# Hybrid two-layer trunk: the first inputs regrouped into one array, fewer and wider first transfers, other first instructions

## The chip, the cores and the metric

The kernel runs on one core of one Trainium2 chip. The metric is device time of one launch in microseconds (us). TensorE is called PE below, VectorE DVE, ScalarE ACT, GpSimd POOL, and SyncE, which issues the transfers, SP.

## The reference

Two layers. Each normalises x, multiplies it with one wide input matrix, runs three kinds of heads on the columns of that product and maps their outputs back by a second matrix into the residual. The sequence has 256 rows, the model 1024 columns; the input matrix has 4360 columns.

```python
def hybrid_layer(x, norm_w, w_in, conv_w, conv_b, gate_bias, ret_norm_w, mlstm_norm_w, w_out):
    h = rmsnorm(x, norm_w)
    proj = jnp.matmul(h, w_in).astype(jnp.float32)
    ...
    (aq, ak, av, ag, bq, bk, bv, bg, cq, ck, cv, co, cg, ci, cf) = jnp.split(proj, cuts, axis=-1)
    ya = moba_attention(split_heads(aq, A_HEADS), ...)   # causal softmax with ALiBi, 8 heads of 64
    ya = merge_heads(ya) * jax.nn.silu(ag)
    yb = retention(rotate(bq, pos), rotate(bk, pos), bv) # 4 heads, decay in place of softmax
    yb = head_norm(yb, ret_norm_w) * jax.nn.silu(bg)
    qk = jax.nn.silu(causal_dwconv(jnp.concatenate([cq, ck], axis=-1), conv_w, conv_b))
    ...
    yc = mlstm(...)                                      # 4 heads, gated matrix memory
    yc = head_norm(yc, mlstm_norm_w) * jax.nn.silu(cg)
    y = jnp.concatenate([ya, yb, yc], axis=-1)
    return x + jnp.matmul(y, w_out)

def reference(x, ...):
    for layer in range(DEPTH):                           # DEPTH = 2
        x = hybrid_layer(x, ...)
    return rmsnorm(x, final_norm_w)
```

## The kernel before

Everything is held in float32. Each operand of a large product is split in two parts that PE multiplies at its fast rate: a rounded part (`hi` of a weight, `xh` of x) and the rest (`lo`, `xl`). Three products, `hi*xh`, `hi*xl` and `lo*xh`, then stand for one. ACT writes the rounded part, DVE subtracts it from the original to get the rest.

x lies transposed: 128 partitions, eight row groups k = 0 to 7 of 256 columns each (the tile `px`, behind 80 columns of small parameters). The weights come in 23 chunks a layer, in the order of use, each some 1 MB, into three `raw` buffers; ACT and DVE split each into one of three `hi` and `lo` buffers. Chunks 0 and 1 (the first four q heads and k heads of the attention) are handled apart: their products for one row group k can start when x's group k and the 256 columns of each chunk that belong to k are there. That is the head of the kernel: 96 products of 256 columns, 12 for each k.

The program's order is written by a small planner, `Sched`, at build time. Each stage (`loader`, `splitter`, `norm`, `project`, the evacuations) is a Python generator; the planner advances the one whose next instruction could start first by its own cost table, and so fixes the order on every engine. Where an instruction is given as `A(...) + V(...)` (the helper `CP`, a copy), the planner picks ACT or DVE by which would end first. The buffers are acquired and released in planner order.

The parts that matter here, with the lines of the profile: `loader` (transfers; the helper `D` on L288 issues them on SP), `first_x` and `first_w` (the split of the first x and weights; ACT on L265, DVE on L259), `norm(0)` (ACT squares pairs of x groups into `t512` buffers, DVE adds them up), `project` (the products; L280), and the preamble on L359 to L372 (memsets, one ACT instruction, two PE products of a zeroed `sb` buffer, whose results nobody reads). `loader` sends the head in 15 transfers: for the row groups 0, 1, 2-3, 4-5, 6-7 one of x and one of each chunk. Behind them on SP stand chunk 2 in two halves, the first table, chunk 3 and so on.

Of the kernel before, what the change touches and what calls it, by code (L numbers as in the profile page):

```python
# [10 lines left out]
F32 = mybir.dt.float32  # L11
# [5 lines left out]
S = 256  # L17
# [36 lines left out]
W_SIZES = [(k1 - k0) * len(c) for _, c, k0, k1 in CHUNKS] + [2048] * 4  # L54
W_OFFS = np.concatenate([[0], np.cumsum(W_SIZES)]).tolist()
W_TOTAL = W_OFFS[-1]


P_NW, P_CW, P_CB, P_GB, P_YW = 0, 16, 48, 56, 72
# [168 lines left out]
@with_exitstack  # L228
def trunk(ctx: ExitStack, tc: tile.TileContext, xp: bass.AP, w: bass.AP, fn: bass.AP,
          tab: bass.AP, out: bass.AP):  # L230
# [65 lines left out]
    def acq(tag):  # L296
        return ("acq", tag)
# [7 lines left out]

    px = sb_tile([128, P_N + KT * S], "px")
    pr = px[:, :P_N]
    x = px[:, P_N:].rearrange("p (k t) -> p k t", t=S)
    tb = sb_tile([128, T_N], "tb")
# [15 lines left out]
    gi = sb_tile([4, 2, S], "gi")  # L325
    on_a = sb_tile([128, 2, 512], "on_a")
    on_b = sb_tile([128, 2, 256], "on_b")
    hc = sb_tile([128, 2, 256], "hc")
    rrow = sb_tile([128, S], "rrow")
# [19 lines left out]
    sb_pool("lo", 3, [128, 2112], F32R)  # L349
    sb_pool("t512", 6, [128, 512])  # L350
    sb_pool("st", 7, [128, 512], F32R)
# [33 lines left out]
    def loader():  # L385
        for i in range(NL):
            l, c = divmod(i, NW)
            n = W_SIZES[c]
            o = l * W_TOTAL + W_OFFS[c]
            if i == 1:  # L390
                continue
            t = yield acq("raw")
            raws[i] = t
            if i < 2:
                if i == 0:
                    t1 = yield acq("raw")
                    raws[1] = t1
                    for a, b in ((0, 1), (1, 2), (2, 4), (4, 6), (6, 8)):
                        o1, o2 = P_N + a * S if a else 0, P_N + b * S
                        e = yield D((o2 - o1) * 512 / 360.0, px[:, o1:o2], xp[:, o1:o2])  # L400
                        for k in range(a, b):
                            sc.set(E("x0", k), e + 1100)
                        for m in range(2):
                            e = yield D((b - a) * 364, (t, t1)[m][:, a * 256:b * 256],
                                        w[:, o + m * 2048 + a * 256:o + m * 2048 + b * 256])
                            for k in range(a, b):
                                sc.set(E("rawk", m, k), e + 1100)
                continue
# [12 lines left out]
        sc.spawn(last_in(), 2)  # L421

    def split_x(l, k):
        wk = pr[:, P_NW + l * 8 + k:P_NW + l * 8 + k + 1]
        yield A(xh[:, k, :], x[:, k, :], AF.Copy, scale=wk)
# [7 lines left out]

    def first_w(m, k):
        yield wait(E("rawk", m, k))
        a = slice(k * 256, (k + 1) * 256)
        yield A(his[m][:, a], raws[m][:, a], AF.Copy)
        t = yield V("tensor_tensor", los[m][:, a], raws[m][:, a], his[m][:, a].bitcast(F32), op=OP.subtract)
        sc.set(E("wk", m, k), t)

    def splitter():
# [3 lines left out]
        for k in range(KT):  # L445
            sc.spawn(first_x(k), -3)
            for m in range(2):
                sc.spawn(first_w(m, k), -2)
        for m in range(2):
            for k in range(KT):  # L450
                yield wait(E("wk", m, k))
            sc.release("raw", raws.pop(m), E("wk", m, KT - 1).time)
        for i in range(2, NL):
# [19 lines left out]
    def norm(l):  # L473

        ss = None
        for k in range(0, KT, 2):
            for z in (k, k + 1):
                yield wait(E("x0", z) if l == 0 else E("res", l - 1, z))
            sq = yield acq("t512")
            yield A(sq, x[:, k:k + 2, :].rearrange("p a t -> p (a t)"), AF.Square)  # L480
# [87 lines left out]
    def project():  # L568
        for l in range(DEPTH):
# [3 lines left out]
            while c < len(CHUNKS):  # L573
# [23 lines left out]
                elif name[1] in "qk":  # L597
# [10 lines left out]
                    hv = [his[q][:, :2048].rearrange("p (k c) -> p k c", k=KT) for q in ii]  # L608
                    lv = [los[q][:, :2048].rearrange("p (k c) -> p k c", k=KT) for q in ii]
                    for k in range(KT):  # L610
                        yield wait(E("x", l, k))
                        for z in range(m):
                            yield wait(E("wk", z, k) if i == 0 else E("w", i + z, k // 4))
                            for t in range(2):
                                cs = slice(t * 128, (t + 1) * 128)
                                for q, (a, b) in enumerate(((hv[z], xh), (hv[z], xl), (lv[z], xh))):
                                    e = yield M(ps[z][:, t * 256:(t + 1) * 256], a[:, k, cs], b[:, k, :],
                                                k + t + q == 0, k == KT - 1 and q == 2)
                    for z, q in enumerate(ii):
# [591 lines left out]
```

## Time and profile before

| | |
|---|---|
| median of three runs (lowest, highest) | 302.06 us (301.41, 302.4) |
| the profiled execution's own time | 301.41 us |
| its span in the trace | 299.6 us |
| PE busy | 291.0 us, 97% of the span |
| DVE busy | 257.7 us, 86% |
| ACT busy | 196.6 us, 66% |
| bytes moved | 48.58 MB, 162 GB/s over the span |

The span runs from the first to the last instruction that the profiler saw; the launch's own time has 1.8 us around it. PE products are pipelined, so that the recorded durations overlap: the distance between two starts tells how fast PE goes, not the duration of one. The same holds, by less, for ACT and DVE.

### The profile page before, as it was taken

To read this page: it belongs to the slowest core of one execution; us is meant where nothing else is said; L and a number is where in the kernel's file an instruction comes from. 1 tells how busy PE (TensorE), PEld (TensorE's weight loads), DVE (VectorE), ACT (ScalarE), POOL (GpSimd) and SP (SyncE) were. 2 spreads that over 40 slices of the span, in tenths; PEclk is the share of its full clock that TensorE was granted. 3 is DMA by queue.
4 is the path that set the end of the run, shared out by engine and by line. 5 is a ranking of instruction groups with operands and counts; after the bars stand their busy time and mean duration, and the time that the engine had idled before them with its cause. 6 is when DMAs were issued, how large, how long until landed. Compare 5 with 4: busy or idle time off the path is not lost.

```text
span 299.6 us, 4795 instructions
## 1 busy us (share of the span) xinstructions
PE 291.0 (97%) x1792; PEld 258.2 (86%) x1792; DVE 257.7 (86%) x549; ACT 196.6 (66%) x341; POOL 15.3 (5%) x19
## 2 busy tenths in 40 slices
PE   8899999999999999999999999999999999999991
PEld 6798989888989888899988898988899988888881
DVE  3969999999999997985679999999999999956353
ACT  5958997889448539644666699779555265845332
POOL 6000000000002002000020000000002002000010
PEclk9999999999999999999999999999999999999997
DMA  6999456574710560754317663446541624330003
GB/s 200 374 398 352 153 174 223 184 258 143 238 45 0 161 240 22 249 174 148 136 19 264 205 222 125 156 142 219 203 142 45 237 67 173 123 131 0 2 0 140
DMA packets 9095, 48.58 MB, mean 162 GB/s; under 512 B 1008, under 2 KB 1904, under 8 KB 4080
## 3 DMA queue, kind: packets, MB, share of 16 engines
q1 hardware_dynamic: 9072, 48.28, 46.7%
q8 instruction: 14, 0.23, 0.3%
q14 instruction: 9, 0.07, 0.1%
HBM read 47.23 MB, written 1.05 MB: 161 GB/s over the span
## 4 chain that ended last, share of the span: by engine, by line
PE 91%; DVE 2%; issue 2%; ACT 1%; DMA 1%; SPq 1%; POOL 0%; POOLq 0%
PE pj L280 71%; PE mx L280 15%; PE mx L285 4%; DMA px<-xp 1%; SPq L288 1%; DVE sb L259 1%; DVE t L259 1%; ACT t L265 0%; ACT hi L265 0%; POOL small L554 0%; ACT xx L265 0%; ACT raw L265 0%; POOLq L1207 0%; DVE raw L259 0%; DVE hc L259 0%
## 5 line engine op out<-in xcount | busy, mean ns | idle before, releaser
L259 DVE TENSOR_TENSOR lo<-raw,hi 128x1024 fp32r<-128x1024 f32 (+2 forms) x96 | 102.8, 1087 | 8.9 <-ACT hi L265 8.7
L265 ACT ACTIVATE hi<-raw 128x1024 fp32r<-128x1024 f32 (+2 forms) x96 | 88.8, 946 | 10.4 <-DMA raw<-w 4.6
L280 PE MATMUL pj<-hi,xx 128*128 128x512 f32 (+1 forms) x320 | 94.4, 374 | 0.0
L280 PE MATMUL pj<-xx,hi 128*128 128x512 f32 (+1 forms) x272 | 88.0, 377 | 0.7 <-ACT hi L265 0.7
L280 PE MATMUL pj<-xx,lo 128*128 128x256 f32 x240 | 68.8, 287 | 0.3 <-DVE lo L259 0.3
L280 PEld LDWEIGHTS pj<-hi,xx 128*128 128x128 f32 x320 | 57.4, 188 | 9.0
L280 PE MATMUL pj<-lo,xx 128*128 128x512 f32 (+1 forms) x160 | 59.4, 371 | 0.0
L280 PEld LDWEIGHTS pj<-xx,hi 128*128 128x128 f32 x272 | 49.9, 192 | 10.1 <-ACT hi L265 1.7
L280 PEld LDWEIGHTS pj<-xx,lo 128*128 128x128 f32 x240 | 45.8, 191 | 0.8 <-DVE lo L259 0.7
L280 PEld LDWEIGHTS pj<-lo,xx 128*128 128x128 f32 x160 | 30.1, 188 | 4.5
L265 ACT ACTIVATE sb<-sb,small 128x128 f32<-128x128 f32 (+1 forms) x48 | 19.5, 448 | 4.9 <-DVE small L259 2.4
L265 ACT ACTIVATE t<-pj 128x256 f32<-128x256 f32 x26 | 9.8, 376 | 17.0 <-PE pj L280 16.9
L265 ACT ACTIVATE st<-t 64x512 fp32r<-64x512 f32 x26 | 16.1, 627 | 4.5 <-DVE t L259 4.2
L1101 POOL TENSOR_TENSOR small<-small,mhalf 128x8 f32<-128x8 f32 x4 | 6.9, 1731 | 181.7 <-DVE small L259 181.7
L280 PE MATMUL pj<-yh,lo 128*128 128x256 f32 x56 | 15.9, 284 | 0.0
L280 PE MATMUL pj<-yh,hi 128*128 128x256 f32 x56 | 15.9, 284 | 0.0
L280 PE MATMUL pj<-yl,hi 128*128 128x256 f32 x56 | 15.8, 283 | 0.0
L280 PE MATMUL mx<-st,st 128*128 128x128 f32 (+1 forms) x64 | 15.1, 270 | 0.0
L265 ACT ACTIVATE t<-pj,small 128x512 f32<-128x512 f32 (+1 forms) x12 | 7.3, 610 | 11.2 <-PE pj L280 11.2
L259 DVE TENSOR_TENSOR t<-pj,t 128x256 f32<-128x256 f32 x26 | 10.9, 419 | 2.2 <-ACT t L265 2.1
L265 ACT ACTIVATE t<-t 32x512 f32<-32x512 f32 (+1 forms) x20 | 12.6, 629 | 0.3
L280 PEld LDWEIGHTS mx<-st,st 128*128 128x128 f32 x64 | 12.1, 189 | 0.6
(150 smaller groups left out, 480.3 us busy)
## 6 DMA issues: line engine op xcount, KB each, us to landing
raw<-w SPq DMA_DIRECT2D x37, 1024.0 KB, 4.8
raw<-w SPq DMA_DIRECT2D x2, 1056.0 KB, 6.2
raw<-w SPq DMA_DIRECT2D x6, 256.0 KB, 5.6
raw<-w SPq DMA_DIRECT2D x2, 512.0 KB, 6.8
tb<-tab SPq DMA_DIRECT2D x1, 960.0 KB, 10.0
px<-xp SPq DMA_DIRECT2D x3, 256.0 KB, 4.8
tb<-tab SPq DMA_DIRECT2D x1, 514.0 KB, 7.7
raw<-w SPq DMA_DIRECT2D x4, 128.0 KB, 2.8
```

What stands on the lines that cost most here:

```text
L259: return op("dve", cost, lambda: getattr(nc.vector, name)(out, *a, **k), after)
L265: return op("act", cost, lambda: nc.scalar.activation(out, in_, func, **k), after)
L280: return op("pe", cost, lambda: nc.tensor.matmul(out, a, b, start=start, stop=stop, skip_group_check=True), after)
L285: return op("pe", 110.0, lambda: nc.tensor.transpose(out, in_, idn))
L288: return op("sp", cost, lambda: nc.sync.dma_start(out, in_))
L1101: yield G(1600, lambda: nc.gpsimd.tensor_tensor(vs, vs, mhalf[:, :8], op=OP.pow))
```

## The change

The first x and the weights of chunks 0 and 1 are put together by row group on the host: the new array `hd` has 80 parameter columns and then, for each k, 256 columns of x, 256 of chunk 0 and 256 of chunk 1 (`H_K` = 768). They land in one tile, which keeps the name `px`. Groups 0 and 1 come in three transfers each, groups 2 to 7 in one each. Chunks 0 and 1 no longer use `raw` buffers, so chunk 2 begins with all three free. The places of the weights in `px` are used again once they are split: those of groups 0 to 3 become four of the six `t512` buffers, those of groups 4 to 7 become `on_b`, `hc` and `on_a`. The split of groups 2 to 7 takes both chunks' 512 columns in one instruction. The first 256 weight columns are rounded on DVE, not ACT. The first twelve products are put in the order in which their operands are made. Seven PE products of a zero constant replace the two of the `sb` buffer, and three POOL memsets shrink to the columns that later instructions do not write.

```diff
+H_K = 256 + 512
...
-    px = sb_tile([128, P_N + KT * S], "px")
+    px = sb_tile([128, P_N + KT * H_K], "px")
     pr = px[:, :P_N]
-    x = px[:, P_N:].rearrange("p (k t) -> p k t", t=S)
+    hx = px[:, P_N:].rearrange("p (k c) -> p k c", c=H_K)
+    x = hx[:, :, 0:S]
...
+    on_b, hc = [hx[:, k, 256:].rearrange("p (b c) -> p b c", b=2) for k in (4, 5)]
+    on_a = hx[:, 6:8, 256:]
...
-    sb_pool("t512", 6, [128, 512])
+    sb_pool("t512", 2, [128, 512])
...
+    zero = nc.const_aps.tensor(0.0, (128, 128), F32)
+    for _ in range(7):
+        nc.tensor.matmul(sc.pools["mx"][0][3][0][:, :128], zero, zero, start=True, stop=True)
...
-    nc.gpsimd.memset(va, 1.0)
-    nc.gpsimd.memset(vc, 1.0)
-    nc.gpsimd.memset(cpad, 0.0)
+    nc.gpsimd.memset(va[:, :, :, HD:], 1.0)
+    nc.gpsimd.memset(vc[:, :, :, HD:], 1.0)
+    nc.gpsimd.memset(cpad[:, :, :3], 0.0)
...
-    dummy = sc.pools["sb"][0][0][0]
-    nc.vector.memset(dummy, 0.0)
-    for _ in range(2):
-        nc.tensor.matmul(sc.pools["mx"][0][3][0][:, :384], dummy[:, :128], dummy, start=True, stop=True)
...
+        for k in range(KT):
+            o = P_N + k * H_K
+            if k < 2:
+                for key, a, b in ((None, o - P_N if k == 0 else o, o + 256), (0, o + 256, o + 512), (1, o + 512, o + 768)):
+                    e = yield D((b - a) * 512 / 360.0, px[:, a:b], hd[:, a:b])
+                    sc.set(E("x0", k) if key is None else E("hw", k, key), e + 1100)
+                continue
+            e = yield D(H_K * 512 / 360.0, px[:, o:o + H_K], hd[:, o:o + H_K])
+            sc.set(E("x0", k), e + 1100)
+            for m in range(2):
+                sc.set(E("hw", k, m), e + 1100)
+        for i in range(2, NL):
...
-                    for a, b in ((0, 1), (1, 2), (2, 4), (4, 6), (6, 8)):
-                        o1, o2 = P_N + a * S if a else 0, P_N + b * S
-                        e = yield D((o2 - o1) * 512 / 360.0, px[:, o1:o2], xp[:, o1:o2])
...
-                            e = yield D((b - a) * 364, (t, t1)[m][:, a * 256:b * 256],
-                                        w[:, o + m * 2048 + a * 256:o + m * 2048 + b * 256])
...
-    def first_w(m, k):
-        yield wait(E("rawk", m, k))
-        a = slice(k * 256, (k + 1) * 256)
-        yield A(his[m][:, a], raws[m][:, a], AF.Copy)
-        t = yield V("tensor_tensor", los[m][:, a], raws[m][:, a], his[m][:, a].bitcast(F32), op=OP.subtract)
-        sc.set(E("wk", m, k), t)
+    def first_w(k, m0, m1):
+
+        h, lo = (t[k // 4][:, k % 4 * 512 + m0 * 256:k % 4 * 512 + m1 * 256] for t in (his, los))
+        r = hx[:, k, 256 + m0 * 256:256 + m1 * 256]
+        yield wait(E("hw", k, m1 - 1))
+        if k + m0 == 0:
+            t = yield V("tensor_copy", h, r, fast=True)
+            sc.set(E("wh"), t)
+        else:
+            yield A(h, r, AF.Copy)
+        t = yield V("tensor_tensor", lo, r, h.bitcast(F32), op=OP.subtract)
+        for m in range(m0, m1):
+            sc.set(E("wk", m, k), t)
+        if k < 4 and m1 == 2:
+            sc.release("t512", hx[:, k, 256:], t)
...
-            for m in range(2):
-                sc.spawn(first_w(m, k), -2)
+            for m0, m1 in ((0, 1), (1, 2)) if k < 2 else ((0, 2),):
+                sc.spawn(first_w(k, m0, m1), -2)
...
+                            qt = [(q, t) for t in range(2) for q in range(3)]
+                            if i + k + z == 0:
+                                yield wait(E("wh"))
+                                qt.sort()
```

The order of the head on SP. Before, `px` is x and `raw_85`, `raw_86` are the weights of chunks 0 and 1; each row is a transfer with its shape:

```order
L288 DMA px<-xp 128x336
L288 DMA raw_85<-w 128x256
L288 DMA raw_86<-w 128x256
L288 DMA px<-xp 128x256
L288 DMA raw_85<-w 128x256
L288 DMA raw_86<-w 128x256
L288 DMA px<-xp 128x512
L288 DMA raw_85<-w 128x512
L288 DMA raw_86<-w 128x512
L288 DMA px<-xp 128x512
```

Of the change, on SP, the whole head and what follows it, with `px` for x and the first weights:

```order
L291 DMA px<-hd 128x336
L291 DMA px<-hd 128x256 x5
L291 DMA px<-hd 128x768 x6
L291 DMA raw_82<-w 128x1024 x2
L291 DMA tb<-tab 128x1028
```

The first six transfers keep their sizes; the nine of 512 columns become six of 768.

The order of the head on DVE before, groups 1 to 3 (`xx` is the rest of x, `lo_91` and `lo_92` the rests of chunks 0 and 1, `t_94` the sum of squares):

```order
L259 SCALAR_TENSOR_TENSOR xx<-px,xx 128x256
L259 TENSOR_TENSOR lo_91<-raw_85,hi_88 128x256
L259 TENSOR_TENSOR lo_92<-raw_86,hi_89 128x256
L259 SCALAR_TENSOR_TENSOR xx<-px,xx 128x256 x2
L259 TENSOR_TENSOR lo_91<-raw_85,hi_88 128x256 x2
L259 TENSOR_TENSOR t_94<-t_94,t_95 128x512
L259 TENSOR_TENSOR lo_92<-raw_86,hi_89 128x256 x2
```

And of the change, on DVE, groups 3 to 5 (`hi_85` and `hi_86` are the rounded parts, `lo_88` and `lo_89` the rests of groups 0 to 3 and 4 to 7, `t_91` the sum of squares):

```order
L262 TENSOR_TENSOR lo_88<-px,hi_85 128x512
L262 TENSOR_TENSOR t_91<-t_91,t_92 128x512
L262 SCALAR_TENSOR_TENSOR xx<-px,xx 128x256
L262 TENSOR_TENSOR lo_89<-px,hi_86 128x512
L262 SCALAR_TENSOR_TENSOR xx<-px,xx 128x256
L262 TENSOR_TENSOR lo_89<-px,hi_86 128x512
```

A group's rest of x and rest of both weights now follow each other, where before two groups' rests of x came first and each chunk's weights behind them.

Further on the planner's choices differ too. Where the first q heads are copied on ACT, into the `st` buffers, before (`t_98` and `t_99` are the evacuated q and k):

```order
L265 ACTIVATE st_102<-t_98 64x512
L265 ACTIVATE st_100<-t_99 64x512
L265 ACTIVATE st_103<-t_98 64x512
L265 ACTIVATE st_101<-t_99 64x512
L265 ACTIVATE st_100<-t_99 64x512
```

And the change at that place on DVE, where the evacuated q and k lie in `px`:

```order
L262 CAST st_96<-px 64x512
L262 TENSOR_TENSOR sr<-tb,rrow 128x256
L262 TENSOR_TENSOR t_92<-pj_114,t_92 128x256
L262 TENSOR_TENSOR sel<-tb 128x512
L262 TENSOR_TENSOR st_95<-px,st_95 64x512
```

Over the first layer DVE has eleven such copies where it had seven, and ACT four fewer; the second layer's order is the same in both.

## Rows read from the trace of the kernel before

**Rows 1.** The page: busy time of each engine, and the chain by engine.
```profile
PE 291.0 (97%) x1792; PEld 258.2 (86%) x1792; DVE 257.7 (86%) x549; ACT 196.6 (66%) x341; POOL 15.3 (5%) x19
...
PE 91%; DVE 2%; issue 2%; ACT 1%; DMA 1%; SPq 1%; POOL 0%; POOLq 0%
```
**Rows 2.** Busy time by stretch: stretch, length, engines (instructions), clock, DMA share, GB/s.
```profile
3.92:8.00 4.08, 4.08 (x25) 4.00 (x24) 2.16 (x6) 2.50 (x6) 1.17 (x3) 1.00 0.91 274
8.00:11.00 3.00, 1.96 (x11) 1.34 (x10) 2.82 (x8) 3.00 (x10) 0.00 (x0) 1.00 0.99 333
11.00:18.50 7.50, 7.50 (x64) 7.50 (x64) 7.50 (x17) 6.46 (x15) 0.00 (x0) 1.00 1.02 394
...
50.00:100.00 50.00, 50.00 (x297) 43.75 (x296) 49.08 (x107) 35.31 (x61) 1.65 (x1) 1.00 0.47 158
100.00:150.00 50.00, 50.00 (x349) 46.32 (x348) 40.69 (x93) 28.99 (x49) 1.64 (x1) 1.00 0.46 156
```
**Rows 3.** The chain of waits in the head: start, length, what.
```profile
3.53 4.08 DMA px<-xp
7.63 0.91 ACT xx L265 x2
...
10.32 0.43 DVE lo L259
...
10.79 10.06 PE pj L280 x76
```
**Rows 4.** PE in order of time: start, duration, line, operation, shapes, count.
```profile
1.37 2.93 PE L372 MATMUL mx<-sb 128*128 128x384 f32 x4 [1.37 <-DVE sb L370]
...
5.28 0.41 PE L280 MATMUL pj<-xx,lo 128*128 128x256 f32 x1
...
5.92 0.41 PE L280 MATMUL pj<-xx,lo 128*128 128x256 f32 x1
...
6.53 0.40 PE L280 MATMUL pj<-xx,hi 128*128 128x256 f32 x2
...
6.89 0.40 PE L280 MATMUL pj<-xx,hi 128*128 128x256 f32 x2
...
7.88 0.29 PE L280 MATMUL pj<-xx,lo 128*128 128x256 f32 x1
8.90 0.50 PE L280 MATMUL pj<-xx,hi 128*128 128x256 f32 x2 [0.73 <-ACT hi L265]
...
18.57 0.40 PE L280 MATMUL pj<-xx,hi 128*128 128x512 f32 x1
```
**Rows 5.** SP's issues of the sixth and the eighth transfer.
```profile
3.05 0.43 SPq L288 DMA_DIRECT2D raw<-w  x1
...
4.00 0.43 SPq L288 DMA_DIRECT2D raw<-w  x1
```
**Rows 6.** Issue to landing (us): the first, fifth, sixth and eighth transfer.
```profile
px<-xp SPq DMA_DIRECT2D x1, 168.0 KB, 2.3
...
raw<-w SPq DMA_DIRECT2D x1, 128.0 KB, 2.7
...
raw<-w SPq DMA_DIRECT2D x1, 128.0 KB, 3.4
...
raw<-w SPq DMA_DIRECT2D x1, 256.0 KB, 4.4
```
**Rows 7.** ACT's square and DVE's work in the head, by time.
```profile
9.06 0.62 ACT L265 ACTIVATE t<-px 128x512 f32<-128x512 f32 x1
...
8.18 0.88 DVE L259 SCALAR_TENSOR_TENSOR xx<-px,xx 128x256 fp32r<-128x256 f32 x2 [0.82 <-ACT xx L265]
...
9.71 0.69 DVE L259 TENSOR_TENSOR t<-t,t 128x512 f32<-128x512 f32 x1
10.32 0.42 DVE L259 TENSOR_TENSOR lo<-raw,hi 128x256 fp32r<-128x256 f32 x1
```
**Rows 8.** DVE's copies by form: names, shapes, count, busy us, mean ns.
```profile
L259 DVE CAST st<-t 64x512 fp32r<-64x512 f32 x22 | 9.2, 420 | 0.4
```

More of the change, by code (lines that the diff above doesn't have):

```diff
@@ L55 @@
 W_OFFS = np.concatenate([[0], np.cumsum(W_SIZES)]).tolist()
+W_HEAD = W_OFFS[2]
 W_TOTAL = W_OFFS[-1]
+H_K = 256 + 512
 P_NW, P_CW, P_CB, P_GB, P_YW = 0, 16, 48, 56, 72
@@ L228, in trunk @@
 @with_exitstack
-def trunk(ctx: ExitStack, tc: tile.TileContext, xp: bass.AP, w: bass.AP, fn: bass.AP,
+def trunk(ctx: ExitStack, tc: tile.TileContext, hd: bass.AP, w: bass.AP, fn: bass.AP,
           tab: bass.AP, out: bass.AP):
@@ L325, in trunk @@
     gi = sb_tile([4, 2, S], "gi")
-    on_a = sb_tile([128, 2, 512], "on_a")
-    on_b = sb_tile([128, 2, 256], "on_b")
-    hc = sb_tile([128, 2, 256], "hc")
+    on_b, hc = [hx[:, k, 256:].rearrange("p (b c) -> p b c", b=2) for k in (4, 5)]
+    on_a = hx[:, 6:8, 256:]
     rrow = sb_tile([128, S], "rrow")
@@ L385, in loader @@
     def loader():
-        for i in range(NL):
+        for k in range(KT):
[10 more added lines that the diff above has]
+        for i in range(2, NL):
             l, c = divmod(i, NW)
             n = W_SIZES[c]
-            o = l * W_TOTAL + W_OFFS[c]
-            if i == 1:
-                continue
+            o = l * W_TOTAL + W_OFFS[c] - W_HEAD
             t = yield acq("raw")
             raws[i] = t
[L394 to L397, printed above, removed]
-                    for a, b in ((0, 1), (1, 2), (2, 4), (4, 6), (6, 8)):
-                        o1, o2 = P_N + a * S if a else 0, P_N + b * S
-                        e = yield D((o2 - o1) * 512 / 360.0, px[:, o1:o2], xp[:, o1:o2])
-                        for k in range(a, b):
-                            sc.set(E("x0", k), e + 1100)
-                        for m in range(2):
-                            e = yield D((b - a) * 364, (t, t1)[m][:, a * 256:b * 256],
-                                        w[:, o + m * 2048 + a * 256:o + m * 2048 + b * 256])
-                            for k in range(a, b):
-                                sc.set(E("rawk", m, k), e + 1100)
-                continue
             m = 2 if i == 2 else 1
@@ L424, in split_x @@
         wk = pr[:, P_NW + l * 8 + k:P_NW + l * 8 + k + 1]
-        yield A(xh[:, k, :], x[:, k, :], AF.Copy, scale=wk)
+        t = yield A(xh[:, k, :], x[:, k, :], AF.Copy, scale=wk)
+        sc.set(E("xh", l, k), t)
         t = yield V("scalar_tensor_tensor", xl[:, k, :], x[:, k, :], wk, xh[:, k, :].bitcast(F32),
@@ L446, in splitter @@
             sc.spawn(first_x(k), -3)
-            for m in range(2):
-                sc.spawn(first_w(m, k), -2)
[L449 to L452, printed above, removed]
+            for m0, m1 in ((0, 1), (1, 2)) if k < 2 else ((0, 2),):
+                sc.spawn(first_w(k, m0, m1), -2)
         for i in range(2, NL):
@@ L479, in norm @@
             sq = yield acq("t512")
-            yield A(sq, x[:, k:k + 2, :].rearrange("p a t -> p (a t)"), AF.Square)
+            yield A(b2(sq), x[:, k:k + 2, :], AF.Square)
             if ss is None:
@@ L607, in project @@
                             yield wait(E("w", q, 0))
-                    hv = [his[q][:, :2048].rearrange("p (k c) -> p k c", k=KT) for q in ii]
-                    lv = [los[q][:, :2048].rearrange("p (k c) -> p k c", k=KT) for q in ii]
+                    if i:
+                        hv, lv = [[t[q][:, :2048].rearrange("p (k c) -> p k c", k=KT) for q in ii] for t in (his, los)]
+                    else:
+                        hv, lv = [[[t[k // 4][:, (k % 4 * 2 + z) * 256:(k % 4 * 2 + z + 1) * 256] for k in range(KT)]
+                                   for z in range(m)] for t in (his, los)]
                     for k in range(KT):
-                        yield wait(E("x", l, k))
+                        yield wait(E("xh" if i + k == 0 else "x", l, k))
                         for z in range(m):
[L613 to L618, printed above, removed]
+                            ak = [v[z][:, k] if i else v[z][k] for v in (hv, lv)]
+                            qt = [(q, t) for t in range(2) for q in range(3)]
+                            if i + k + z == 0:
+                                yield wait(E("wh"))
+                                qt.sort()
+                            else:
+                                yield wait(E("wk", z, k) if i == 0 else E("w", i + z, k // 4))
+                            for q, t in qt:
+                                a, b = ((ak[0], xh), (ak[0], xl), (ak[1], xh))[q]
+                                if i + k + z == 0 and q:
+                                    yield wait(E("x", l, k) if q == 1 else E("wk", z, k))
+                                e = yield M(ps[z][:, t * 256:(t + 1) * 256], a[:, t * 128:(t + 1) * 128], b[:, k, :],
+                                            k + t + q == 0, k == KT - 1 and q == 2)
                     for z, q in enumerate(ii):
@@ L1183 @@
     x, w_in, w_out = f(x), f(w_in), f(w_out)
-    xT = x[0].T.reshape(KT, 128, S).transpose(1, 0, 2).reshape(128, KT * S)
+    xT = x[0].T.reshape(KT, 128, S).transpose(1, 0, 2)
     w = np.empty((128, DEPTH * W_TOTAL), np.float32)
@@ L1201 @@
     fn = np.ascontiguousarray(np.broadcast_to(f(final_norm_w), (128, D_)))
-    ins = {"xp": np.concatenate([par, xT], 1), "w": w, "fn": fn, "tab": _tables()}
+    head = np.concatenate([xT, w[:, :2048].reshape(128, KT, 256), w[:, 2048:W_HEAD].reshape(128, KT, 256)], 2)
+    ins = {"hd": np.concatenate([par, head.reshape(128, -1)], 1), "w": np.ascontiguousarray(w[:, W_HEAD:]), "fn": fn,
+           "tab": _tables()}
     nc = _bacc.Bacc("TRN2", target_bir_lowering=False, num_devices=1)
```

## The prediction

> **What bounds the kernel now.** I read the page's busy shares and its chain first, then the busy time by stretch, then the chain of waits and PE's own order inside the one stretch where PE is idle. PE is busy 97% of the span and is 91% of the chain [rows 1]. By stretch it is busy for all of 11 to 18.5 and of 50 to 150 us; between 8 and 11 us it is busy for 1.96 of 3.00 us [rows 2]. So the only thing to win ahead of the tail is in the head, and a change that does not make PE's products fewer can give back no more than PE's idle time there, plus what PE does slowly at the start.
>
> The chain tells what that idle time waits for [rows 3]: the transfer of x's groups 2 and 3 (issued 3.53, landed 7.61), ACT's rounding from 7.63, DVE's rest of a weight at 10.32, and from 10.79 on PE without a break. PE's rows agree: it ends row group 1 with a product at 7.88 and starts group 2 at 8.90, released by ACT [rows 4]. Chunk 2 begins at 18.57, and that moment is what the change can move: behind it PE is full. Each product takes 0.12 us there (three in the 0.36 us from 6.53 to 6.89); from 5.28 to 5.92 three took 0.64 us [rows 4]. [...]
>
> **The change, part by part.**
>
> *The start.* The seven dummies are 896 columns for 768; four recorded pieces of the latter stood from 1.37 for 2.93 us [rows 4]. They no longer wait for a DVE memset, so they begin some 0.6 us sooner and end near where they did. The rounding of the first weights on DVE beside ACT's first x, the new order of the first twelve products, and the groups 0 and 1 in single pieces all act on groups 0 and 1. These 24 products end at 7.88 + 0.12 = 8.00 now, 0.9 us before group 2 can start, and that idle time hides them. I take nothing for all of them. At most they could cost or give that 0.9 us if group 2 came as soon as they end. The smaller POOL memsets: POOL has no work behind 8 us in the head [rows 2] and none of its results is in the chain; nothing.
>
> *The transfers.* The first six keep size and place, so I let them land as now: the sixth is issued at 3.05 and lands 3.4 us later, at 6.45 [rows 5, 6]. The seventh, issued at 3.53, now holds all of group 2: 384 KB in place of 256 KB of x. What is wanted is its landing, L, which no row shows. Before, the 256 KB issued at that place landed at 7.61 [rows 3], and with the next 256 KB (issued 4.00, 4.4 us) the first 512 KB were there at 8.40 [rows 5, 6]. 384 KB lie half way, 8.0. The bytes come in rows of 3 KB a partition where they were 2 KB, and by stretch the rate rises from 274 GB/s (mostly 1 KB and 2 KB rows) to 394 (up to 4 KB) [rows 2]. So L lies between 7.61 and 8.40; I take 7.8.
>
> *From L to chunk 2.* ACT starts 0.02 us after a landing and starts a second x 0.42 after the first (0.91 for two less one of 0.49) [rows 3]. The 512 weight columns in one instruction stand for two of 256; the nearest ACT row is the square of 512 columns, 0.62 us, and the nearest DVE row an add of 512, 0.69 [rows 7]. With 0.04 us for each hand-over (10.75 to 10.79 [rows 3]), the rest of group 2's weights is there at L + 0.02 + 0.42 + 0.62 + 0.04 + 0.69 + 0.04 = L + 1.83. PE has done the first two products of group 2 by then (they need only the rounded weights), and has 70 of the 96 left: 8.40 us. Checked on before: at 10.79 it has 64 left, which gives 18.47 where 18.57 is recorded, so I add 0.10. Chunk 2 starts at L + 10.33: 18.13 with L = 7.8, that is 0.44 us sooner; 17.94 (0.63 sooner) with 7.61, 18.73 (0.16 later) with 8.40.
>
> *Whether the supply keeps up.* From group 2 on, DVE starts follow each other by 0.40 us after a rest of x (0.88 for two less one of 0.48) and 0.61 after 512 columns [rows 7]. In the new order it needs five rests of weights, five of x and two adds from the start of group 2's rest to the start of group 7's: 5 x 0.61 + 5 x 0.40 + 2 x 0.61 = 6.27, so this one ends at L + 1.10 + 6.27 + 0.69 = L + 8.1; PE asks for it at about L + 9.1. Group 6's ends at L + 7.5 and is asked for at L + 7.7. So PE stays full, but by 0.2 us in the tightest place; if 512 columns take 0.05 us more than the add shows, group 6 and 7 wait a little, and the gain shrinks by some 0.2. In the new order group 3 and later are needed 1.44 us apart (12 x 0.12) and land about 1.0 to 1.1 us apart, so that their landing is hidden.
>
> *Behind the head.* Chunk 2 and the following chunks find three free `raw` buffers, and are issued earlier. PE does not wait for them now, so nothing comes of it; it is their cover if PE asks sooner. The order of the first layer differs after the head: four copies of 64 x 512 go from ACT to DVE, 4 x 0.42 = 1.68 us [rows 8], in a stretch where DVE is busy for 49.08 of 50 us (50 to 100) [rows 2]. It has 9.3 us of slack in the 50 us after that. Between nothing (PE has work that does not need DVE) and 1.68 us (all of it reaches PE) I take nothing, since PE has not one wait in that stretch now and two engines feed it in turn; the other end is a rival below.
>
> *The sum.* The profiled execution took 301.41 us, 299.6 of span and 1.8 around it; minus 0.44 that is 300.97. It was the lowest of the three, 0.65 under their median, and a median is forecast: 302.06 - 0.44 = 301.6.
>
> **The rivals.**
>
> *Third group without a queue (faster).* The fifth transfer landed 2.7 us after its issue, the sixth after 3.4 and the seventh after 4.1 [rows 3, 6]: a queue builds up. If larger rows and fewer transfers keep it from doing so, the sixth lands at 3.05 + 2.7 = 5.75, and 384 KB at the 394 GB/s of 11 to 18.5 us [rows 2] take 1.0 us more: L = 6.75, chunk 2 at 17.08, 1.5 us sooner, 300.6 us. For it: nine transfers become six. Against it: DMA is at 0.91 to 0.99 of its share in 3.92 to 11 us [rows 2], so that it is bytes and not issues that wait, and the rows of the first six are as short as before.
> [...]
>
> *DVE becomes the bound in the first layer (slower).* If the 1.68 us of copies all reach PE in the stretch where DVE is full, the kernel loses 1.68 - 0.44 = 1.2 us: 303.3. It is slower than before from 0.44 us on, a quarter of the copies' time. For it: 49.08 of 50 us [rows 2]. Against it: DVE does less in the head (sixteen rests of 256 columns become four and six of 512), and PE begins this stretch with no wait at all.
>
> [...]
>
> *It doesn't do what it says.* If 384 KB land as late as the 512 KB did or later (8.4), the head ends where it did, and the time is 302.1.
>
> **How the numbers follow.** A measurement of this kernel tells some 0.3%, 0.9 us, from no change. The forecast, 0.0 to 0.8 us gained, has 0.50, nearly all of it within that bound; 0.04 of it may read faster by the spread of the runs. The larger gain has 0.27, of which 0.24 is beyond the bound. Slower by DVE 0.13 and by the clock 0.04, together 0.16 beyond the bound with what else may stall. No change at all has 0.06. That makes faster 0.28, same 0.56, slower 0.16. The range reaches to the larger gain and to most of the DVE case: 300.4 to 302.8; the forecast's own is 301.2 to 302.2.
>
> **What would show it.** In the profile of the changed kernel: the seventh transfer's landing near 7.8 and chunk 2's first product near 18.1; PE without idle time from the third product of group 2 on; the 512-column roundings at 0.62 us on ACT and the rests at 0.69 on DVE; no PE wait for DVE between 50 and 100 us. The forecast is wrong if group 2 lands before 7.3 or after 8.4, if PE waits for DVE's rests in groups 4 to 7, or if PE is idle anywhere between 20 and 250 us.

## The result, and the profile after

The changed kernel is slower: 303.32 us median (302.95 to 305.26, 8 runs) against 301.87 (300.97 to 302.64, 8 runs), a ratio of 1.0053 with a 95% interval of 1.0028 to 1.0078. By the ratio 1.6 us are lost, by the medians 1.45, where 0.4 gained was forecast. The profiled execution took 303.27 us with a span of 301.5. Times below are medians, and ratios go against runs of the kernel before on the same chip. One execution of the first single move below, at 326.52 us and a mean granted clock of 0.846, is far off its others and left out of its median.

The page of the kernel after, busy time and chain by engine; both answer to [rows 1]:

```profile
PE 292.5 (97%) x1802; PEld 260.3 (86%) x1802; DVE 258.6 (86%) x547; ACT 193.9 (64%) x330; POOL 13.4 (4%) x19
...
PE 86%; ACT 4%; DVE 3%; issue 2%; DMA 2%; SPq 1%; POOL 0%; POOLq 0%
```

PE is as full as before by its share, but the chain no longer is PE's for 91%: ACT has gone from 1% to 4%. Something on ACT now sets the pace somewhere. The busy time by stretch says where (columns as in [rows 2]):

```profile
3.92:8.00 4.08, 4.08 (x24) 3.68 (x24) 2.19 (x6) 2.13 (x5) 0.00 (x0) 1.00 0.93 287
8.00:11.00 3.00, 1.80 (x13) 1.40 (x13) 2.19 (x5) 2.76 (x6) 0.00 (x0) 1.00 1.02 363
11.00:18.50 7.50, 7.50 (x65) 7.50 (x64) 7.50 (x14) 6.38 (x12) 0.00 (x0) 1.00 1.03 412
50.00:100.00 50.00, 49.42 (x277) 42.18 (x276) 47.00 (x108) 34.52 (x59) 1.89 (x1) 1.00 0.47 164
100.00:150.00 50.00, 50.00 (x358) 46.78 (x357) 42.72 (x99) 27.45 (x50) 1.64 (x1) 1.00 0.44 148
```

The head did not improve: PE is busy for 1.80 of 3.00 us in 8 to 11, before it was 1.96. And PE now has idle time in 50 to 100 us, 0.58 us, where it had none; DVE is less busy there than before (47.00 for 49.08). So there are two questions: why the head gained nothing, and what stops PE behind it.

The head first. The chain of waits of the kernel after, in the same place as [rows 3]:

```profile
3.52 4.70 DMA px<-hd
...
8.24 0.51 ACT xx L268
8.74 0.53 ACT hi L268
...
9.30 0.70 DVE lo L262
```

Group 2's 384 KB were issued at 3.52 and landed at 8.22. From there all goes as worked out: 512 columns take 0.6 us on ACT and 0.7 on DVE. PE in order of time, in the head, near 75 us, and at a product of the second layer:

```profile
8.07 0.28 PE L283 MATMUL pj<-xx,lo 128*128 128x256 f32 x1
9.32 0.50 PE L283 MATMUL pj<-xx,hi 128*128 128x256 f32 x2 [0.97 <-ACT hi L268]
...
18.55 0.40 PE L283 MATMUL pj<-xx,hi 128*128 128x512 f32 x1
...
75.02 0.39 PE L283 MATMUL pj<-xx,hi 128*128 128x512 f32 x1
75.99 3.02 PE L283 MATMUL mx<-va,et 128*128 128x65 f32 x24 [0.58 <-ACT va L268]
...
154.08 0.40 PE L283 MATMUL pj<-xx,hi 128*128 128x512 f32 x1
```

Chunk 2 starts at 18.55; before it was 18.57 [rows 4]. At 75.99 PE waits for ACT's `va`, the values of the attention. The same two places in the kernel before, which were not shown:

```profile
75.76 2.79 PE L280 MATMUL mx<-va,et 128*128 128x65 f32 x24
...
152.41 0.40 PE L280 MATMUL pj<-xx,hi 128*128 128x512 f32 x1
```

There is no wait at 75.76. The product that starts at 152.41 before starts at 154.08 after, 1.67 us later: the whole loss is there by then. Counted by the columns that PE has multiplied, since the attention's products come in another order, the lag is at most 0.4 us up to 74 us (0.17 there) and 1.5 us at 83. Why `va` is late stands in ACT's rows, first of after, then of before:

```profile
67.64 1.28 ACT L268 ACT_TABLE_LOAD   x1
68.94 0.21 ACT L268 ACTIVATE small<-small 128x8 f32<-128x8 f32 x1
...
70.76 1.28 ACT L268 ACT_TABLE_LOAD   x1
72.05 0.64 ACT L268 ACTIVATE t<-px 128x512 f32<-128x512 f32 x1
72.70 0.63 ACT L268 ACTIVATE st<-px 64x512 fp32r<-64x512 f32 x1
73.36 2.01 ACT L268 ACTIVATE hi<-raw 128x1024 fp32r<-128x1024 f32 x2
75.27 1.24 ACT L268 ACTIVATE va<-pj,small 128x512 f32<-128x512 f32 x2
```

```profile
69.83 2.01 ACT L265 ACTIVATE hi<-raw 128x1024 fp32r<-128x1024 f32 x2
71.86 1.28 ACT L265 ACT_TABLE_LOAD   x1
73.16 0.21 ACT L265 ACTIVATE small<-small 128x8 f32<-128x8 f32 x1
73.27 1.25 ACT L265 ACTIVATE va<-pj,small 128x512 f32<-128x512 f32 x2
```

The `small` row of 128x8 is the Ln of the gates (`evac_cv`). It needs another function table than the tanhs of the convolution: a load of 1.28 us stands ahead of it in both kernels (67.64 and 71.86), and in after another ahead of the tanh that follows it (70.76). Before, both tanhs were done ahead of it, and `va` came right behind it, at 73.27. After, the Ln (the expectations below call it the layer norm's; it is the gates') stands between the two tanhs, so a second load, 1.28 us, comes ahead of the second tanh, then two roundings of 2.0 us, and `va` comes at 75.27. The number of loads in the kernel is the same, five; one has moved in front of something that PE waits for.

### The profile page after: what moved, and what is told of

It is laid out like the page before. It is cut to its first block, busy times and chain, and to the rows that moved or that the text cites. A ratio compares the mean times of both kernels' runs of the same rounds, so it can differ in the third digit from the quotient of the medians.

```text
span 301.5 us, 4795 instructions
## 1 busy us (share of the span) xinstructions
PE 292.5 (97%) x1802; PEld 260.3 (86%) x1802; DVE 258.6 (86%) x547; ACT 193.9 (64%) x330; POOL 13.4 (4%) x19
## 4 chain that ended last, share of the span: by engine, by line
PE 86%; ACT 4%; DVE 3%; issue 2%; DMA 2%; SPq 1%; POOL 0%; POOLq 0%
PE pj L283 67%; PE mx L283 15%; PE mx L288 4%; DMA px<-hd 2%; ACT hi L268 2%; DVE lo L262 1%; ACT L268 1%; SPq L291 1%; DVE sb L262 1%; DVE t L262 1%; DVE px L262 1%; ACT px L268 0%; POOL small L556 0%; ACT sb L268 0%; ACT raw L268 0%
## 5 line engine op out<-in xcount | busy, mean ns | idle before, releaser
L262 DVE TENSOR_TENSOR lo<-raw,hi 128x1024 fp32r<-128x1024 f32 (+1 forms) x80 | 96.5, 1218 | 6.7 <-ACT hi L268 6.4
L268 ACT ACTIVATE hi<-raw 128x1024 fp32r<-128x1024 f32 (+1 forms) x80 | 83.0, 1054 | 7.2 <-issue 2.9
L268 ACT ACTIVATE px<-pj 128x256 f32<-128x256 f32 x22 | 8.3, 378 | 22.0 <-PE pj L283 21.9
L268 ACT ACTIVATE px<-px 128x512 f32<-128x512 f32 (+1 forms) x13 | 8.2, 629 | 12.0 <-DVE px L262 12.0
L262 DVE SCALAR_TENSOR_TENSOR px<-cpad,px 128x256 f32<-128x256 f32 x24 | 11.3, 480 | 1.8 <-ACT px L268 1.6
L283 PEld LDWEIGHTS mx<-va,et 128*128 128x128 f32 x96 | 11.6, 192 | 1.2 <-ACT va L268 0.9
L283 PE MATMUL mx<-va,et 128*128 128x65 f32 x96 | 11.9, 273 | 0.6 <-ACT va L268 0.6
```

Source lines behind the costliest of these rows:

```text
L262: return op("dve", cost, lambda: getattr(nc.vector, name)(out, *a, **k), after)
L268: return op("act", cost, lambda: nc.scalar.activation(out, in_, func, **k), after)
L283: return op("pe", cost, lambda: nc.tensor.matmul(out, a, b, start=start, stop=stop, skip_group_check=True), after)
```

## The experiments

*The order behind the head, or the head itself?* The planner's order of each kernel was recorded, and a kernel made that follows a stored order in place of choosing. So the head of one could be put in front of the order of the other.

```diff
     def run(self):
-        while self.live:
-            best = None
...
+        for key, eng in order_of():
+            th = next(th for th in self.live if th.key == key)
```

The head of after, the order of before behind it:

> The changed kernel's head with all its edits (pieces, tile, DVE rounding of the first weights, dummies, memsets); everything behind the head is issued in the order, and on the engines, that the kernel before had there. Theory 1 (the loss is made by the order that the planner found behind the new head: the layer norm's Ln between the two tanhs of the convolution, so that a table load and two roundings of 2.0 us stand in ACT's queue ahead of the evacuations of va): the wait of PE for va near 75 us is gone and the time is the kernel before's, 301.9 +- 0.3, since chunk 2 starts at the same 18.55. Theory 2 (the new head itself costs the time: its tiles, or four copies fewer on ACT): 303.3, with the products of the second layer still 1.6 us late.

301.72 us, ratio 0.9996 (0.9976 to 1.0016). The head of before, the order of after behind it:

> The mirror: the kernel before's head, and behind it the order and the engines of the changed kernel. Theory 1 (order behind the head): 303.3 +- 0.4, with PE waiting near 75 us for ACT's evacuation of va. Theory 2 (the new head itself): 301.9.

303.39 us, ratio 1.0057 (1.0038 to 1.0077), with PE waiting 0.6 us for `va`. The new layout, its tiles and the dummies cost nothing that this interval shows; the order costs the loss. No line of the diff asks for that order: it is what the planner finds when the head's instructions and times are others (the last run below finds the old one again, but for the places of one rounding and its rest near 16 us).

*What in the order?* Two single moves in the order of after. The first takes the two roundings that stand ahead of `va` and puts them behind it:

```diff
 ACT: st<-px 64x512
-     hi<-raw 128x1024 x2
      va<-pj,small 128x512 x2
+     hi<-raw 128x1024 x2
```

> The changed kernel with one move in its order: the two roundings of chunk 12 on ACT, and the rests that go with them, stand behind the two evacuations of va instead of ahead of them. Theory 1: va comes about 2 us sooner on ACT, PE's wait at 75.0 to 76.0 goes, and what the roundings now come late for is small: 302.3 to 302.6, that is 0.7 to 1.0 us of the 1.5 us lost. Theory 2 (DVE, with the four copies that it took over, is what PE waits for in the first layer): no change, 303.3.

305.98 us, ratio 1.0152 (1.0106 to 1.0197): much worse, and against theory 1 as I had put it. The move was also less than the expectation says: in the trace only ACT's order differs from that of after, while DVE's rests of those roundings stand where they stood. The rows show what follows, DVE's first and then PE's:

```profile
75.91 2.36 DVE L300 TENSOR_TENSOR lo<-raw,hi 128x1024 fp32r<-128x1024 f32 x2 [1.84 <-ACT hi L306]
...
79.69 0.55 DVE L300 TENSOR_TENSOR et<-mx,tb 128x384 f32<-128x384 f32 x1
```

```profile
75.57 2.79 PE L321 MATMUL mx<-va,et 128*128 128x65 f32 x24
80.30 0.39 PE L321 MATMUL mx<-st,st 128*128 128x256 f32 x1 [1.94 <-DVE et L300]
...
81.58 0.63 PE L321 MATMUL pj<-xx,hi 128*128 128x512 f32 x1
```

`va` was no longer late. But in DVE's order the rests of those roundings stand ahead of `et`, a tile of the attention that PE multiplies with the values: DVE waited 1.84 us for ACT, and PE then 1.94 us for `et`. PE's products were slow right behind that idle time (one of 512 columns took 0.63 us at 81.58, where it takes 0.39 at 75.02 in after; the granted clock of 50 to 100 us is 0.97). So at this place two things wait for ACT: `va`, and the roundings by way of DVE. The second move leaves the roundings and puts the Ln behind the second tanh:

```diff
-ACT_TABLE_LOAD
-small<-small 128x8           (Ln)
 hi<-raw 128x1024
 st<-px 64x512
-ACT_TABLE_LOAD
 t<-px 128x512                (second tanh)
+ACT_TABLE_LOAD
+small<-small 128x8           (Ln)
```

> The changed kernel with one move in its order: the Ln of the layer norm stands behind the second tanh of the convolution, so that the table load that lies ahead of that tanh comes after it; the number of loads stays the same. Theory 1: ACT's queue up to va is shorter by one table load, 1.28 us, va comes that much sooner and PE's wait of 0.6 to 1.0 us near 75 us goes: 302.2 to 302.6. Theory 2 (DVE bounds the first layer): no change, 303.3.

ACT's rows now:

```profile
69.09 0.64 ACT L306 ACTIVATE t<-px 128x512 f32<-128x512 f32 x1
69.73 1.28 ACT L306 ACT_TABLE_LOAD   x1
...
73.81 1.25 ACT L306 ACTIVATE va<-pj,small 128x512 f32<-128x512 f32 x2
```

In the trace `va` came at 73.81 and PE's wait for it was gone; the product of 152.41 started at 153.25, 0.83 us sooner than in after. But the median, 303.10 (ratio 1.0046, 1.0024 to 1.0068), hardly moved from after's 1.0053. It was settled later on a head whose runs scatter less (only group 0 in single pieces, explained below):

> The head with only group 0 in single pieces (300.48 with the order of before behind it, its runs within 0.7 us of each other), and behind it the order of the changed kernel. Theory 1 (the order alone costs what was lost behind the head): the same head, 1.5 to 1.7 us later from va near 75 us on: 302.1 +- 0.3. Theory 2 (the order is only bad together with a late head): 300.5 to 301.0.

> As the run before, with the Ln behind the second tanh. With a head that varies less, what the move is worth can be told: the trace of the first try showed PE 0.8 us sooner behind va, its median hardly 0.2. If the trace is right: 0.8 us under the run with the changed kernel's order, 301.3. If the median is right: 0.2 under it, 301.9.

302.43 us (1.0027, 1.0010 to 1.0045) and 301.66 us (1.0007, 0.9992 to 1.0022). With the order of before that head takes 300.48 on another chip (0.9962, below). So the order costs some 2.0 us there, and the place of the Ln 0.8 of it: the trace was right. Of the remaining 1.2 us some 0.8 arise between 73 and 90 us by the traces. There the waits of the last kernel show PEld, PE's weight loads, waiting for DVE (us in total, times, longest):

```profile
PEld mx L321 <- DVE et L300: 0.3, 1, 0.3
PEld mx L321 <- DVE px L300: 0.2, 1, 0.2
```

That part was not taken away in a run of its own, so its cause stays open: these 0.5 us point to DVE, and other moves in the order are as possible.

*Why did the head gain nothing?* With the order of before behind the head, the number of groups in single pieces was changed (after has 2; a group in single pieces is three transfers of 128 KB, x and the two weights, and the first has the parameters with it):

```diff
-            if k < 2:
+            if k < 1:        # or 4, or 8
...
-            for m0, m1 in ((0, 1), (1, 2)) if k < 2 else ((0, 2),):
+            for m0, m1 in ((0, 1), (1, 2)) if k < 1 else ((0, 2),):
```

> As the run with the new head and the order of before behind it, but groups 0 to 3 come in single pieces (x, weights of aq0, weights of ak0), groups 4 to 7 as one transfer each. Theory A (the head waits for the landing of the whole 384 KB piece of group 2): x of group 2 lands near 7.0 to 7.2 and its weights near 7.7 and 8.2, PE starts group 2 at about 8.4 in place of 9.0 to 9.3 and chunk 2 some 0.6 to 0.9 us sooner; 300.8 to 301.2. Theory B (bytes set the pace: what the pieces give early, the later groups take back, since their landings are as late): PE waits in groups 3 to 6 instead, chunk 2 at 18.5 to 19.0, 301.4 to 302.0.

> The same with all eight groups in single pieces: 24 transfers of 128 KB, each issued 0.5 us behind the one before, so the last is issued at 12.5 us. Theory A (landing of the whole piece of group 2): as with four groups in pieces, 300.8 to 301.2, since the last piece still lands at 15.5 and is asked for at about 17. Theory B (the rate of the queue sets the pace, and rows of 1 KB are slower): the rate of 11 to 18.5 us falls from 424 GB/s, PE waits in groups 5 to 7, 302.0 to 303.0.

> The other way: only group 0 in single pieces, groups 1 to 7 as one transfer each. Theory A: group 1 comes late as a whole, near 6.8, so PE starts it at about 7.7 in place of 6.5 and the two roundings of it stand in front of group 2's; chunk 2 at 18.5 to 19.0: 301.5 to 302.2. Theory B (fewer short rows move the bytes faster): group 2 lands at 7.5, and chunk 2 starts near 18.0: 301.2.

Four groups: 301.42 us (0.9989, 0.9973 to 1.0005). Eight: 303.48 us (1.0071, 1.0045 to 1.0097). One: 300.48 us (0.9962, 0.9948 to 0.9975). Theory A is out: more pieces start group 2 sooner (8.60 with four) and lose it again behind. One group in pieces is even better than theory B had it (301.2). SP's issues and the stretches of the kernel with eight groups in pieces show the pace:

```profile
0.73 11.29 SPq L330 DMA_DIRECT2D px<-hd  x24
...
3.92:8.00 4.08, 3.76 (x21) 3.56 (x20) 2.37 (x7) 2.88 (x8) 0.00 (x0) 1.00 0.90 269
8.00:11.00 3.00, 2.95 (x25) 2.75 (x25) 2.90 (x9) 2.69 (x8) 0.00 (x0) 1.00 0.90 259
```

SP issues one transfer per 0.47 us (24 in 11.29 us; in after at 2.09, 2.57, 3.04, 3.52). Pieces of 128 KB at that pace are 279 GB/s, and 259 to 269 are moved. Each piece lands 2.2 to 3.6 us after its issue, the last, issued at 11.59, after 3.0: no queue of bytes builds up, too few bytes are issued. The DMA share of these rows is 0.90 all the same, so a share near 1 does not show that bytes wait. With 384 KB per issue the same queue moves 363 to 412 GB/s in after. Still, short rows could be the reason too. Two runs for that. In the first, group 1's whole transfer is cut into three across the partitions, so that rows stay long and issues become more:

```diff
-            e = yield D(H_K * 512 / 360.0, px[:, o:o + H_K], hd[:, o:o + H_K])
+            for a, b in ((0, 48), (48, 96), (96, 128)) if k == 1 else ((0, 128),):
+                e = yield D(H_K * (b - a) * 4 / 360.0, px[a:b, o:o + H_K], hd[a:b, o:o + H_K])
```

> As with only group 0 in single pieces, but group 1's transfer is cut across the partitions into three (48, 48 and 32 partitions), so that there are twelve transfers as in the changed kernel, with rows of 3 KB as in the better one. Theory R (the length of the rows sets the rate): group 2 lands near 7.1 as there, 300.5 to 300.8. Theory N (the number of transfers, each with its issue of 0.5 us, sets when group 2 comes): its transfer is issued 1.0 us later and lands at 7.9 to 8.3: 301.4 to 301.7.

302.27 us (1.0014, 0.9998 to 1.0030): theory N. Group 1 was complete at 6.56 in place of 5.82, group 2 at 8.3. The time is above what N expected, and the rows say why (stretch, then PE):

```profile
8.00:11.00 3.00, 2.78 (x14) 2.57 (x14) 2.56 (x6) 2.93 (x7) 0.00 (x0) 0.57 1.00 317
```

```profile
6.15 0.28 PE L321 MATMUL pj<-xx,lo 128*128 128x256 f32 x1
7.75 0.50 PE L321 MATMUL pj<-xx,hi 128*128 128x256 f32 x2 [1.33 <-ACT hi L306]
...
8.86 0.63 PE L321 MATMUL pj<-xx,hi 128*128 128x256 f32 x2
```

Behind an idle time of 1.33 us the granted clock is 0.57 in 8 to 11 us, and two products take 0.43 us from 8.86 on in place of 0.24. In six of its twelve executions the mean granted clock is 0.990 or 0.991, and they took 302.3 to 302.8 us; the other six, at 0.994 to 0.998, took 301.1 to 302.2. In the second run, pieces and rows are those of after, but ACT issues group 1's three, beside SP:

```diff
+    for z in range(3):
+        a = P_N + H_K + z * 256
+        nc.scalar.dma_start(px[:, a:a + 256], hd[:, a:a + 256])
     nc.vector.memset(ones, 1.0)
...
-                    e = yield D((b - a) * 512 / 360.0, px[:, a:b], hd[:, a:b])
+                    if k == 0:
+                        e = yield D((b - a) * 512 / 360.0, px[:, a:b], hd[:, a:b])
```

> The changed kernel's head, groups 0 and 1 in single pieces of the same sizes and rows, the order of before behind it, but the three pieces of group 1 are issued by ACT ahead of its first activation, beside SP, which goes from the three pieces of group 0 straight to group 2. Theory I (SP issues one transfer per 0.47 us, so that 128 KB pieces feed the queue with 275 GB/s at most and group 2 is issued as late as 3.52): group 2 is issued at 2.1 and lands near 6.7 to 7.2 in place of 7.9 to 8.5; ACT's first rounding is some 0.3 us later by its three issues; chunk 2 at 17.6 to 17.9, 300.5 to 300.9. Theory R (short rows are what is slow, whoever issues them): group 2 lands at 7.9 or later, 301.4 to 301.8.

301.39 us (0.9988, 0.9970 to 1.0006). The issue of group 2 at 2.1 (KB, us to landing) and PE's first product:

```profile
px<-hd SPq DMA_DIRECT2D x1, 384.0 KB, 4.9
```

```profile
4.82 1.20 PE L322 MATMUL pj<-xx,hi 128*128 128x256 f32 x4 [0.72 <-DVE hi L301]
```

Group 2 landed at 7.0, as theory I had it, with short rows. ACT's transfers also have a queue of their own in the trace (q10 beside SP's q1), so that this run does not tell the pace of the issues from the gain of a second queue. Yet the kernel was no faster. Its first product came late, at 4.82, and PE then needed 0.64 us for three products until 9.7, where it needs 0.36 from about 6 on elsewhere. The same was seen with no group in pieces at all, and eight transfers:

```diff
-            if k < 2:
...
-            e = yield D(H_K * 512 / 360.0, px[:, o:o + H_K], hd[:, o:o + H_K])
+            a = o if k else 0
+            e = yield D(H_K * 512 / 360.0, px[:, a:o + H_K], hd[:, a:o + H_K])
```

> No group in pieces: the parameters and group 0 are one transfer of 424 KB, eight transfers in all, the order of before behind the head. Theory C (long rows move the bytes faster, and group 2's landing is what counts): DMA of 3.92 to 8 us stays near 350 GB/s or rises, group 2 lands 0.2 to 0.4 us sooner than 7.1, but group 0 lands at about 4.2 in place of 3.0, PE's first product is 1 us later and the first two groups run back to back into group 2: between 0.3 us faster and 0.5 us slower than with group 0 in pieces (300.2 to 301.0). Rival (late first product costs PE its fast clock as well): 301.5 or more.

300.66 us (0.9961, 0.9943 to 0.9979). That is inside theory C's range, but group 2 landed at 7.14, no sooner than with group 0 in pieces. Its PE rows:

```profile
0.77 3.33 PE L403 MATMUL mx<-const-float32-0.0 128*128 128x128 f32 x14 [0.77 <-PEq L1252]
4.64 1.44 PE L321 MATMUL pj<-xx,hi 128*128 128x256 f32 x4 [0.54 <-ACT xx L306]
...
6.31 0.63 PE L321 MATMUL pj<-xx,hi 128*128 128x256 f32 x2
...
8.23 0.63 PE L321 MATMUL pj<-xx,hi 128*128 128x256 f32 x2
```

PE stood idle for 0.54 us between the dummies and the first product. Two more dummies fill that:

```diff
-    for _ in range(7):
+    for _ in range(9):
```

> As with no group in pieces, but nine dummies in place of seven, so that PE is busy from 0.77 until the first product at 4.64. There PE stood idle for 0.54 us behind the dummies, and its products then took 0.21 us each until 8.8, where they take 0.12 us from 5.5 on in the kernels without that gap. Theory G (the gap is what costs PE its fast level): 24 products of groups 0 and 1 end near 8.0 in place of 9.1, chunk 2 starts some 0.5 to 0.9 us sooner than without, 299.8 to 300.2. Theory H (the fast level comes with the number of true products, whatever stands ahead): no change, 300.66.

> As with group 1's three pieces issued by ACT, but nine dummies in place of seven. There group 2 landed at 7.0, as theory I had it, but the first product came at 4.82, 0.72 us behind the dummies, and PE ran its first 36 products at 0.21 us each. Theory G (the gap costs the fast level): chunk 2 starts 0.6 to 1.0 us sooner, 300.4 to 300.8, and the landing of group 2 that the two issuing queues give is seen in the time. Theory H: 301.4.

With no group in pieces 299.89 us (0.9942, 0.9923 to 0.9962), with two issuing engines 300.77 us (0.9972, 0.9961 to 0.9982): inside theory G's ranges, and theory H is out. The gap does not cost in every execution: the eleven times with seven dummies and no group in pieces fall in two groups, four of 299.5 to 299.9 us and seven of 300.6 to 301.3, and all six with nine dummies are 299.75 to 300.01. Only one of the seven was traced. Nor do these runs tell the closed gap from the larger number of products ahead of the first true one. PE with no group in pieces and nine dummies:

```profile
0.77 4.06 PE L403 MATMUL mx<-const-float32-0.0 128*128 128x128 f32 x18 [0.77 <-PEq L1252]
4.75 1.15 PE L321 MATMUL pj<-xx,hi 128*128 128x256 f32 x4
...
6.33 0.40 PE L321 MATMUL pj<-xx,hi 128*128 128x256 f32 x2
6.57 0.28 PE L321 MATMUL pj<-xx,lo 128*128 128x256 f32 x1
6.69 0.40 PE L321 MATMUL pj<-xx,hi 128*128 128x256 f32 x2
...
17.32 0.40 PE L321 MATMUL pj<-xx,hi 128*128 128x512 f32 x1
```

Three products take 0.36 us from 6 us on, and chunk 2 starts at 17.32, 1.25 us sooner than before. This kernel is the fastest of all. Two more runs: the start edits alone in the kernel before, and the changed kernel with only the number of groups in pieces set to 1, its planner free to choose (the diff above, no stored order).

```diff
+    for _ in range(7):
+        nc.tensor.matmul(sc.pools["mx"][0][3][0][:, :128], zero, zero, start=True, stop=True)
-    nc.gpsimd.memset(va, 1.0)
+    nc.gpsimd.memset(va[:, :, :, HD:], 1.0)
...
-    for _ in range(2):
-        nc.tensor.matmul(sc.pools["mx"][0][3][0][:, :384], dummy[:, :128], dummy, start=True, stop=True)
```

> The kernel before with the start edits alone: seven dummy products of 128 columns from the constant in place of two of 384, no memset of the dummy on DVE, and the memsets of va, vc and cpad cut to the columns that are wanted. Prediction: 0.0 +- 0.2 us (301.7), because PE is idle ahead of group 2 in any case. Rival (the start of PE's fast stretch counts): 0.3 us or more faster.

> The changed kernel with one number changed: only group 0 comes in single pieces; its planner chooses the order by itself. It puts both tanhs of the convolution ahead of the Ln, as before, so the wait for va near 75 us should not come: 300.5 +- 0.3, as with the replayed order of before. If the order that the planner finds here has a stall of its own: above 301.0.

The first: 301.43 us (0.9998, 0.9984 to 1.0011), nothing, as costed. The second: 300.49 us (0.9967, 0.9954 to 0.9981); the planner put both tanhs ahead of the Ln again, and PE has no wait for `va`.

## Why the prediction was wrong

By the traces the head missed its forecast by 0.42 us (chunk 2 at 18.55 for 18.13), and what stands behind it by 1.7 us (PE's lag goes from -0.02 us at chunk 2 to 1.67 at 152 us).

*What bounds the kernel: right.* PE, and in the head the landing of group 2; what the head gains would have reached the end, as the last runs show (1.0 and 1.25 us sooner at chunk 2, 1.1 and 1.5 in the time).

*The start and the memsets at nothing: right*, by a run of their own (ratio 0.9998).

*The landing L: the mis-sized term.* I took 7.8, it was 8.22 in the profiled run; in three others of the same head 7.92, 8.06 and 8.52. The bounds, 7.61 to 8.40, held three of the four. The gain of 0.44 us went with it. I kept the first six transfers "as now" and asked only how the seventh's bytes would fare, and put the 274 GB/s of that stretch down to short rows [rows 2]. The runs point to SP's issue pace times 128 KB, 279 GB/s: with short rows from two engines the same transfer landed at 7.0. The rows for the pace were there: SP's issues are 0.47 us apart [rows 5].

*From L to chunk 2, L + 10.33: right.* 8.22 gives 18.55, and 18.55 is recorded; two more traces with this head have 8.06 and 18.39, 8.52 and 18.86. *That the supply keeps up: right* where later landings are even. In the run of that head with the order of before, group 3 took 5.84 us to land and PE waited again, so that chunk 2 began at 19.09 with group 2 at 7.92: the landing of the later groups is hidden by little.

*Behind the head, the reorder at nothing: the step that failed.* It made the result slower: this term cost 1.7 us in the exchange of heads (303.39 for 301.72) and 2.0 us on the head with one group in pieces. The sign that I had given for it, PE idle between 20 and 250 us, is what showed. The order that the planner writes for the changed kernel had the Ln between the tanhs and two roundings ahead of `va`; I looked at four copies that went from ACT to DVE and not at what stood in ACT's queue ahead of a tile that PE waits for. "PE has not one wait in that stretch now" said nothing on how near a wait was: with `va` done at 74.5 and asked for at 75.76, there were 1.2 us of slack, and the new order took 2.0. The Ln's place is 0.8 us of the cost; the rest is not shown.

*The rival "DVE becomes the bound in the first layer"* gave 303.3, which is the time measured, but this is luck for the part that the runs explain. In 50 to 100 us DVE was less busy than before, not fuller (47.00 for 49.08 us), and what it lacks there it did in the next 50 us (42.72 for 40.69); PE's wait at 75.99 is for ACT. The two runs with heads exchanged do not tell the two apart, since the four copies go with the order. The move of the Ln does, for 0.8 us. For the remaining 1.2 us, where PE's weight loads wait for DVE, this rival is not excluded.

*The rival "third group without a queue"* (1.5 us, 300.6) named a real gain and bound it to the wrong edit: it needs fewer transfers ahead of group 2 than this change leaves. What I held against it was a wrong reading: a DMA share of 0.91 to 0.99 was to show that bytes wait and not issues, and 0.90 stands where issues set the pace. Eight transfers of 384 KB (the first 424) in place of twenty-four of 128 KB (the first 168) take 3.6 us less here, of which 0.8 needed two more dummies.

*Slower by the clock, 0.04:* no run shows the term behind this chance; it was the author's estimate. What the runs showed in its place: in the profiled execution the granted clock reads 1.00 through the idle time ahead of 9.32, in the experiment with the cut transfer 0.57 in 8 to 11 us. A lower clock is not excluded for every execution of this kernel: two of the eight show a mean granted clock of 0.991 and took 304.54 and 305.26 us, the other six 0.995 to 0.997 and 302.95 to 303.76. Of the kernel before, ten of 128 executions show 0.988 to 0.990 and took 302.9 to 303.5 us. None of these was traced, so where their clock fell is not shown.

## What to carry to other kernels

Where a planner or a greedy scheduler writes the order, a change of its input times is a change of all that follows: compare the new order on each engine with the old one, at every tile that the bounding engine waits for, and give the slack there in us, not the absence of a wait. Small first transfers feed a queue no faster than they are issued (here one per 0.47 us, 279 GB/s at 128 KB): count bytes per issue before asking for bandwidth, and do not take a high DMA share for waiting bytes (here 0.90 at 259 to 269 GB/s). And when an earlier landing comes with a later first product, look at what that costs: here an idle time of 0.54 or 0.72 us ahead of it went with 4 to 5 us in which three products took 0.64 us, and two dummies more took the ratio from 0.9961 to 0.9942 and from 0.9988 to 0.9972.

## What the runs showed of the hardware that was not expected

SP's first eleven issues in after are 0.47 us apart (0.73 to 5.42) whether they carry 128 or 384 KB, and the twelfth came 1.04 us behind the eleventh; 128 KB per 0.47 us is 279 GB/s. The DMA share reads 0.90 at the 259 to 269 GB/s of such pieces, and 1.02 at 363. Twelve transfers from two engines land group 2 at 7.0 where twelve from one land it at 8.2.

In the two traces with an idle time of 0.54 or 0.72 us between the dummies and the first product, three products took 0.64 us for the 4 to 5 us from that product on, until 8.7 and 9.7, with a granted clock of 1.00 in the column; with two dummies more three took 0.36 us from 6.0 and 6.5 us on.
